# Order of heads and hyena channels, and where six modulation vectors are computed, in a two-layer hybrid mixer

## The chip, the cores and the metric

The kernel runs on one core of a Trainium2 chip. Its engines work beside each other: PE (TensorE) multiplies matrices into PSUM, DVE (VectorE), ACT (ScalarE) and POOL (GpSimd) do element work, and SP (SyncE) issues the DMAs that bring the weights from HBM. Each engine takes its own instructions in the order in which the program gives them and waits for the others by semaphores. The metric is the device time of one execution in microseconds (us), median of three runs.

## What is computed

Two layers over 256 latent and 256 context tokens of width 1024. Each layer has a token mixer of three branches and a mixture of 16 experts. Shift, scale and gate vectors (six per layer) come from a matrix product of two condition vectors with `w_mod`.

```python
mod  = split((sc     @ w_mod + b_mod), 6)     # latent tokens
modc = split( sc_ctx @ w_mod + b_mod,  6)     # context tokens
h    = modulate(rmsnorm(x, norm1_g), mod[0], mod[1])
dq, dk, dv, hy, sq, sk, sv, gt = split_in(h @ w_in)
y_diff = differential attention over dq, dk, dv      # 8 heads
y_hy   = hyena(hy): short conv, then FFT convolution with a computed filter
y_swa  = windowed attention with a sink over sq, sk, sv
y  = (sum of sigmoid(gate_b) * (y_b @ w_branch[b]) over the three branches) @ w_out
x  = x + mod[2] * y
h2 = modulate(rmsnorm(x, norm2_g), mod[3], mod[4])
x  = x + mod[5] * experts(h2)                        # top-k tokens of each expert
```

The second layer needs only the latent tokens behind its projections. A final RMSNorm closes the program.

## The kernel before, in words

The activations lie transposed in SBUF, channels on the partitions and tokens along the rows: 512 columns in the first layer, 256 (512 for keys and values) in the second.

**Blocks.** A mixer is a list of 116 blocks, made by `mixer` (L1371) and run by `run_blocks` (L984). A block is one slice of 128 columns of `w_in`, `w_branch` or `w_out`, loaded as `wraw` by SP, split into a high part `wh` (ACT) and a low part `wl` (half on POOL, half on DVE, L962), and multiplied with the high and low parts of its input (`hhi`, `hlo`, or `yb`, `mg`): 8 pieces of three matmuls (L456 and L459). The order of the list is: 24 blocks of heads (`diff_in`, L1418: q, k, v of each of 8 heads), 24 of hyena (`hyena_in`, L1403), four of the window attention (`swa_in`, L1477), then for each branch eight pairs of gate block and branch block (`branch`, L1428) with the other eight window blocks strewn in, and eight of the output. A block's last step (`evac`) takes the result from PSUM into a slot of the arena, a pool of SBUF slots, and may start a background task.

**Background tasks.** Each head, each hyena channel group and each window is a Python generator (`diff_gen` L1094, `hyena_gen` L1252, `swa_gen` L1189). `Background` (L286) keeps a queue of them, four live in the first layer and three in the second. Between the pieces of a block, `pump` (L366) steps those that its own clock model holds ready, as long as a credit of PE time lasts and ACT and DVE are not too far behind. All this happens while the program is built; what comes out is a fixed order for each engine. Two things force tasks without credit: `slot` (L391), where the arena has no free slot, and `drain` (L398), at a gate. The gates are the first block of each branch, whose `pre` (L1429) needs all tasks of its group finished, splits their results into `yb` and frees their slots. Before, the first gate drains heads and hyena together, and the first hyena block drains the task `filter` (L847), which computes the first layer's hyena filter in the background. Each hyena task reads that filter (`K`) and the transform matrices (`dft`) that follow it.

**Modulation vectors.** Vectors 0 and 1 of the first layer are computed in the setup. `mod_run` (L707) computes five more, (0,2), (0,3), (0,4), (1,0), (1,1) as (layer, vector), in the background of the first mixer: it loads 128 rows of 1024 columns of `w_mod` into `wm` and multiplies them on PE, four matmuls of 256 columns side by side in the array, 8 such groups a vector. Vector (0,5) is computed in the same way by a task that the fifth output block starts (`modA`, L1558) and that the expert stage drains (L1887). In the second mixer `mod_vec` (L727) computes three vectors on DVE instead: `ma = wm * sc + ma` for 8 pieces, and then four matmuls on PE that sum over the partitions by a selection matrix. `MODR` (L45) says how many blocks before the end of the second mixer this starts.

**Expert stages.** The weights of 16 experts come in pieces of 2 MB (`mw`) into buffers that the mixer gives up near its end and that the experts give back.

Of the kernel before, what the change touches and what calls it, by code (L numbers as in the profile page):

```python
# [17 lines left out]
OP = mybir.AluOpType  # L18
AX = mybir.AxisListType

D = 1024
KT = 8
# [13 lines left out]
COST = {"setup": 500.0, "filter": 60000.0, "mod": 15000.0, "modA": 5000.0, "modN": 5000.0, "diff": 9000.0, "hy": 10000.0, "swa": 4000.0, "post": 1000.0}  # L36
# [8 lines left out]
MODR = 58  # L45
# [8 lines left out]
MAGIC = 12582912.0  # L54
PI_IN = 3.1415925
# [352 lines left out]
class Kernel:  # L408
# [298 lines left out]
    def mod_run(self, vs, depth, pause, delay=3000.0):  # L707
        todo = [(l, v, k) for l, v in vs for k in range(KT)]
        raw = deque(self.mod_load(*todo.pop(0)) for _ in range(depth))
        yield wait(raw[0], delay=delay)  # L710
        for l, v in vs:
            acc = self.bank([128, 256], "m")
            for k in range(KT):
                w = raw.popleft()
                for c in range(4):
                    self.mm(acc[c * 32:(c + 1) * 32, :], self.sc[:, k, :], w[:, c * 256:(c + 1) * 256], k == 0, k == KT - 1, 4)
                w = None
                if todo:
                    yield wait(gate=self.room(a4=1))
                if todo:  # L720
                    raw.append(self.mod_load(*todo.pop(0)))
                yield wait(*list(raw)[:1], delay=pause)
            yield wait(acc, bank=0)
            yield from self.mod_out(l, v, acc)
            yield from self.mod_post(l, v)

    def mod_vec(self, vs):  # L727
        for l, v in vs:
# [19 lines left out]
            acc = None  # L748
            yield wait(p, bank=0)
            yield from self.mod_out(l, v, p, 30)  # L750
            yield from self.mod_post(l, v)
# [232 lines left out]
    def run_blocks(self, bl, ahead=2, first=3):  # L984
        nl = ns = first
        later = []
        for j, b in enumerate(bl):
# [11 lines left out]
            if self.bg.layer and len(bl) - 1 - j == MODR:  # L999
                self.bg.add("mod", lambda task: self.mod_vec([(1, v) for v in range(3, 6)]))  # L1000
# [251 lines left out]
    def hyena_gen(self, task, l, cs, u3):  # L1252
# [5 lines left out]
        yield wait(uv, gate=self.room(a2=2))  # L1258
# [112 lines left out]
    def mixer(self, l):  # L1371
# [28 lines left out]
        def pre_hy():  # L1400
            self.bg.drain("filter")

        def hyena_in():  # L1403
            w = 3 - ns
            for c0 in range(0, KT, w):
                cs = list(range(c0, c0 + w))
                for j in range(3):
                    for i, c in enumerate(cs):
                        def ev_c(p, cs=cs, c=c, i=i, j=j):
# [5 lines left out]
                        add(cols(win, O_HY + j * D + c * 128), H, nt, ev_c,  # L1415
                            *((pre_hy, ("filter",)) if c == 0 and j == 0 else ()))
# [11 lines left out]
        def branch(b, first, group):  # L1428
            def pre():  # L1429
# [3 lines left out]
                if first:  # L1433
                    self.bg.drain("hy")
                    self.K.pop(l)
                    self.dft = None
# [558 lines left out]
```

## Time and profile before

| what | value |
|---|---|
| median of three runs | 2637.61 us (2637.21 to 2639.09) |
| the profiled execution | 2639.09 us |
| its span, first to last instruction | 2637.3 us |
| PE busy | 2244.6 us, 85% |
| DVE busy | 1332.7 us, 51% |
| ACT busy | 883.4 us, 33% |
| POOL busy | 786.9 us, 30% |
| HBM read | 584.66 MB |
| mean granted TensorE clock | 0.937 |

The table gives the whole span; the shares are means over four stages: the first mixer (to about 1010 us), its experts (to 1544), the second mixer (to 2147), its experts. A share of busy time says little here. What a stage is bound by is read from the table of stretches below: which engine is near the length of the stretch, and whether the DMA share is near 1. In it a number in brackets with x counts instructions, and PEld is PE's loading of weights. PEclk is the mean of the clock granted to PE over the stretch, as a share of 2.4 GHz.

### The profile page before, as it was taken

Reading aid. Unit: us, or ns where it says so; the run is one execution under the profiler, and the core shown is the slowest. Engines: PE = TensorE matmul, PEld = TensorE weight load, DVE = VectorE, ACT = ScalarE, POOL = GpSimd, SP = SyncE. Lnnn points to the kernel's source line nnn. Section 1 sums busy time; section 2 is a strip of 40 time slices with the busy share of each in tenths; the row PEclk is TensorE's granted clock in tenths of the full one; section 3 lists DMA queues with packets and bytes.
Section 4 is the critical chain, followed back from the end, with each engine's and each line's share of the span. In section 5 each row is a group of like instructions: output and inputs, shape, how many; then the busy total and the mean of one; then the engine's idle time right before and its main releaser. Section 6 shows DMA issues by size and latency. Waiting matters only on the chain.

```text
span 2637.3 us, 38629 instructions
## 1 busy us (share of the span) xinstructions
PE 2244.6 (85%) x14938; PEld 1534.3 (58%) x14938; DVE 1332.7 (51%) x2899; ACT 883.4 (33%) x1933; POOL 786.9 (30%) x775
## 2 busy tenths in 40 slices
PE   6999998889989998898989799898888987666565
PEld 4777776767768774333333277787777863232223
DVE  4777788867662324223342158778788541111111
ACT  4445653345552332101110056553554430000001
POOL 2654225642333440001110055446554630000000
PEclk8999998989999999999999999998899988777888
DMA  8433342111213377999999942242365889999998
GB/s 293 119 120 112 96 128 89 52 53 52 69 57 88 92 251 288 373 407 400 356 379 403 404 158 80 72 121 80 100 180 160 253 308 409 409 409 409 409 409 305
DMA packets 390239, 590.31 MB, mean 224 GB/s; under 512 B 45948, under 2 KB 278056, under 8 KB 388776
## 3 DMA queue, kind: packets, MB, share of 16 engines
q1 hardware_dynamic: 390056, 587.84, 62.6%
q8 instruction: 118, 1.93, 0.3%
q14 instruction: 65, 0.53, 0.1%
HBM read 584.66 MB, written 3.15 MB: 223 GB/s over the span
## 4 chain that ended last, share of the span: by engine, by line
PE 40%; DMA 16%; DVE 13%; issue 3%; ACT 2%; SPq 2%; POOL 1%; ACTq 0%; DVEq 0%; POOLq 0%
PE p L457 38%; DMA mw<-in_moe_w_dram 15%; DVE t L260 3%; DVE arena L260 3%; PE p L468 2%; SPq L260 2%; DVE wl L260 2%; DVE qp L260 1%; DVE yb L260 1%; ACT wh L260 1%; ACT arena L260 1%; DVE ma L260 0%; DMA wraw<-in_w_in_dram 0%; DVE s L260 0%; DVE aT L260 0%
## 5 line engine op out<-in xcount | busy, mean ns | idle before, releaser
L457 PE MATMUL p<-mw,xg 128*32 128x256 f32 (+1 forms) x3072 | 406.7, 514 | 120.2 <-DMA mw<-in_moe_w_dram 120.0
L457 PE MATMUL p<-hhi,wh 128*128 128x512 f32 (+1 forms) x1344 | 496.7, 370 | 11.1 <-DVE arena L260 8.2
L457 PE MATMUL p<-hhi,wl 128*128 128x512 f32 (+1 forms) x1344 | 481.4, 358 | 26.9 <-DVE wl L260 26.4
L457 PE MATMUL p<-hlo,wh 128*128 128x512 f32 (+1 forms) x1344 | 476.6, 355 | 2.5 <-POOL hlo L260 1.4
L260 POOL TENSOR_TENSOR wl<-wraw,wh 128x512 fp32r<-128x512 f32 x232 | 330.9, 1427 | 460.2 <-ACT wh L260 365.9
L457 PEld LDWEIGHTS p<-mw,xg 128*32 128x32 f32 (+1 forms) x3072 | 137.3, 132 | 331.7 <-issue 203.7
L457 PEld LDWEIGHTS p<-hhi,wl 128*128 128x128 f32 x1344 | 258.3, 192 | 76.6 <-DVE wl L260 41.8
L457 PEld LDWEIGHTS p<-hhi,wh 128*128 128x128 f32 x1344 | 259.0, 193 | 49.3 <-issue 17.7
L457 PEld LDWEIGHTS p<-hlo,wh 128*128 128x128 f32 x1344 | 259.2, 193 | 30.3 <-POOL hlo L260 2.0
L260 ACT ACTIVATE wh<-wraw 128x1024 fp32r<-128x1024 f32 x232 | 242.1, 1053 | 43.2 <-PE p L457 12.1
L457 PE MATMUL p<-mw,aT 128*32 128x256 f32 (+3 forms) x1760 | 204.0, 483 | 59.3 <-DMA mw<-in_moe_w_dram 42.4
L260 DVE TENSOR_TENSOR wl<-wraw,wh 128x512 fp32r<-128x512 f32 x231 | 195.5, 846 | 60.1 <-ACT wh L260 58.9
L260 ACT ACTIVATE arena<-p 128x512 f32<-128x512 f32 (+1 forms) x212 | 106.0, 504 | 344.7 <-PE p L457 286.2
L260 ACT ACTIVATE yS<-p 32x256 f32<-32x256 f32 (+2 forms) x84 | 35.2, 419 | 499.3 <-PE p L457 465.8
L457 PE MATMUL p<-yb,wh 128*128 128x512 f32 (+1 forms) x768 | 197.1, 347 | 0.0
L260 POOL TENSOR_TENSOR sq<-sq,sq 128x512 f32<-128x512 f32 (+1 forms) x6 | 6.4, 1058 | 577.3 <-ACT sq L260 575.4
L457 PEld LDWEIGHTS p<-mw,aT 128*32 128x32 f32 (+1 forms) x1760 | 78.0, 134 | 167.9 <-issue 86.5
L260 DVE TENSOR_TENSOR s<-s,p 128x512 f32<-128x512 f32 (+1 forms) x32 | 17.7, 554 | 290.2 <-PE p L457 290.1
L260 DVE COPY yS<-p 32x512 f32<-32x512 f32 (+1 forms) x60 | 33.3, 556 | 244.5 <-ACT yS L260 244.5
L457 PE MATMUL p<-yb,wl 128*128 128x512 f32 (+1 forms) x384 | 133.2, 347 | 17.4 <-DVE wl L260 16.3
L457 PEld LDWEIGHTS p<-yb,wh 128*128 128x128 f32 x768 | 133.3, 195 | 15.0 <-issue 1.2
L260 ACT ACTIVATE arena<-p,t 128x512 f32<-128x512 f32 (+1 forms) x192 | 116.3, 612 | 65.2 <-DVE t L260 59.2
(235 smaller groups left out, 3506.0 us busy)
## 6 DMA issues: line engine op xcount, KB each, us to landing
mw<-in_moe_w_dram SPq DMA_DIRECT2D x173, 2048.0 KB, 19.3
wraw<-in_w_in_dram SPq DMA_DIRECT2D x152, 512.0 KB, 4.0
wm<-in_w_mod_dram SPq DMA_DIRECT2D x72, 512.0 KB, 4.5
mw<-in_moe_w_dram SPq DMA_DIRECT2D x40, 512.0 KB, 15.8
mw<-in_moe_w_dram SPq DMA_DIRECT2D x17, 1024.0 KB, 21.4
wraw<-in_w_branch_dram SPq DMA_DIRECT2D x32, 512.0 KB, 3.9
wm<-in_w_mod_dram SPq DMA_DIRECT2D x5, 2048.0 KB, 8.1
wraw<-in_w_in_dram SPq DMA_DIRECT2D x32, 256.0 KB, 3.3
```

Source lines behind the costliest of these rows:

```text
L260: return f(*args, **kw)
L457: self.nc.tensor.matmul(out, lhsT=lhsT, rhs=rhs, start=start, stop=stop, skip_group_check=tiles > 1)
L468: self.nc.tensor.transpose(out, in_, self.ident[:n, :n])
```

## The change

Three things change, all in the program that makes the order.

1. The blocks of heads and of hyena channels are dealt in turn by a table `ORDER`, one letter per head (`d`) or hyena group (`h`). In the first layer four heads come first, then `hhd hhd hhhh dd`; in the second they alternate, with four heads at the end. The hyena branch becomes the first of the three branches and the heads' branch the second, so that the first gate drains only hyena. The first hyena block no longer drains the filter; a hyena task itself waits until filter and transform matrices are there.
2. `mod_run` and its two tasks are gone. A new `mod_both` computes the vectors (0,2) to (0,5), (1,0) and (1,1) on DVE, in halves of 512 columns, for both condition vectors; it starts 62 blocks before the end of the first mixer.
3. The costs `modA` and `modN` and the two drains of these tasks are gone.

```diff
-MODR = 58
+MODR = (62, 58)
+ORDER = ("dddd" + "hhd" * 2 + "hhhh" + "dd", "dh" * 4 + "dddd")
...
-    def mod_run(self, vs, depth, pause, delay=3000.0):
...
-                for c in range(4):
-                    self.mm(acc[c * 32:(c + 1) * 32, :], self.sc[:, k, :], w[:, c * 256:(c + 1) * 256], k == 0, k == KT - 1, 4)
...
+    def mod_both(self, vs):
+        for l, v in vs:
+            p = None
+            for hf in range(2):
+                def load(k):
+                    t = self.sb("a2", [128, 512], name="wm")
+                    self.nc.sync.dma_start(t, self.A["w_mod"][l, k * 128:(k + 1) * 128, v * D + hf * 512:v * D + hf * 512 + 512])
+                    return t
+
+                yield wait(gate=self.room(a4=1, a2=3), bank=0)
+                acc = self.sb("a4", [128, 2, 512], name="ma")
+                ws = deque(load(k) for k in range(2))
+                for k in range(KT):
+                    yield wait(ws[0], acc, bank=0)
+                    w = ws.popleft()
+                    for s in range(2):
+                        sc = self.sc[:, k, s:s + 1]
+                        if k:
+                            self.stt(acc[:, s], w, sc, acc[:, s], OP.mult, OP.add)
+                        else:
+                            self.ts(acc[:, s], w, sc, None, OP.mult)
...
+                        self.mm(p[q * 32:(q + 1) * 32, :], self.sel[s], acc[:, s, c * 256:(c + 1) * 256], s == 0, s == 1, 4)
...
-            if self.bg.layer and len(bl) - 1 - j == MODR:
-                self.bg.add("mod", lambda task: self.mod_vec([(1, v) for v in range(3, 6)]))
+            if len(bl) - 1 - j == MODR[self.bg.layer]:
+                vs = [(1, v) for v in range(3, 6)] if self.bg.layer else [(0, v) for v in range(2, 6)] + [(1, 0), (1, 1)]
+                self.bg.add("mod", lambda task: (self.mod_vec if self.bg.layer else self.mod_both)(vs))
...
-        yield wait(uv, gate=self.room(a2=2))
+        yield wait(uv, gate=lambda: l in self.K and len(self.dft or ()) == 2 and self.room(a2=2)())
...
-        diff_in()
-        hyena_in()
+        parts = {"d": diff_in(), "h": hyena_in()}
+        for c in ORDER[l]:
+            next(parts[c])
...
-        branch(0, True, "diff")
-        branch(1, False, "hy")
+        branch(1, True, "hy")
+        branch(0, False, "diff")
...
-                if j == 4 and full:
-                    vs = [(l, 5)]
-                    self.bg.add("modA", lambda task: self.mod_run(vs, 2, 1300.0, 19000.0 if full else 11000.0))
...
-            self.bg.drain("modA")
...
-        self.bg.add("modN", lambda task: self.mod_run([(0, 2), (0, 3), (0, 4), (1, 0), (1, 1)], 1, 6000.0))
```

What this does to the order of the engines is seen at three places. In the names, `arena` is a slot, `ma` the accumulator of a modulation vector, `qp` a split query, `svt` transposed values, `t` a small statistic. First PE in the fifteenth block of the first mixer, before:

```order
L457 MATMUL p_1298<-wm_1303,sc_121 32x256 x4
L468 MATMUL p_1428<-cst_68,arena_576 128x128 x2
L457 MATMUL p_1421<-hhi_337,wh_1354 128x512
L457 MATMUL p_1421<-hlo_338,wh_1354 128x512
L457 MATMUL p_1421<-hhi_337,wl_1355 128x512
```

and now:

```order
L458 MATMUL p_1334<-kp_868,qp_1025 128x512
L458 MATMUL p_1334<-kl_869,qp_1025 128x512
L458 MATMUL p_1330<-hhi_337,wh_1241 128x512
L458 MATMUL p_1330<-hlo_338,wh_1241 128x512
L458 MATMUL p_1330<-hhi_337,wl_1242 128x512
```

The groups on `wm` have left the early blocks; there was about one in each.

Second DVE around block 66 of the first mixer, where the window tasks run, before:

```order
L260 TENSOR_TENSOR wl_6140<-wraw_5871,wh_6139 128x512
L260 SCALAR_TENSOR_TENSOR arena_87<-arena_87,p_6143 128x512
L260 TENSOR_TENSOR wl_6174<-wraw_5962,wh_6173 128x512
L260 STREAM_SHUFFLE sh_6206<-arena_574 128x256
L260 TENSOR_TENSOR arena_574<-arena_574,cst_68 128x256
L260 TENSOR_TENSOR wl_6212<-wraw_6095,wh_6211 128x512
```

and now:

```order
L261 COPY arena_574<-p_5910 128x128
L261 SCALAR_TENSOR_TENSOR ma_5748<-wm_5871,sc_121,ma_5748 128x512 x2
L261 COPY arena_572<-p_5920 128x512
L261 SCALAR_TENSOR_TENSOR ma_5748<-wm_5908,sc_121,ma_5748 128x512 x2
L261 TENSOR_REDUCE t_5960<-p_5941 128x1
L261 TENSOR_REDUCE t_5960<-p_5942 128x1
L261 TENSOR_TENSOR t_5960<-t_5960,nsink_409 128x2
L261 TENSOR_TENSOR t_5960<-t_5960,sink_408 128x2
L261 COPY arena_572<-p_5951 128x128
L261 TENSOR_TENSOR qp_5884<-arena_572,qp_5884 64x128 x2
L261 SCALAR_TENSOR_TENSOR ma_5748<-wm_5935,sc_121,ma_5748 128x512 x2
L261 TENSOR_TENSOR wl_5904<-wraw_5710,wh_5903 128x512
```

Accumulations of `ma` now stand between the steps of the window tasks, ahead of the next block's `wl`.

Third DVE at the gate of the third branch in the second mixer, between the evacuations of the blocks before and behind it, before:

```order
L260 SCALAR_TENSOR_TENSOR arena_11572<-arena_11572,p_16923 128x256
L260 TENSOR_TENSOR yb_16960<-arena_11573,yb_16960 128x256 x4
L260 TENSOR_TENSOR wl_16957<-wraw_16907,wh_16956 128x512
L260 SCALAR_TENSOR_TENSOR ma_16517<-wm_16933,sc_121,ma_16517 128x1024
L260 TENSOR_TENSOR wl_17012<-wraw_16946,wh_17011 128x512
```

and now, of which the first twelve rows of some sixty ahead of `yb` stand here:

```order
L261 SCALAR_TENSOR_TENSOR arena_11728<-arena_11728,p_16775 128x256
L261 TENSOR_TENSOR t_16716<-t_16716 128x2
L261 RECIPROCAL t_16716<-t_16716 128x2
L261 TENSOR_SCALAR arena_11728<-arena_11728,t_16716 128x512
L261 TENSOR_SCALAR arena_11729<-arena_11729,t_16716 128x512
L261 TENSOR_TENSOR qp_16721<-arena_11729,qp_16721 64x128 x2
L261 COPY arena_11728<-p_16832 128x128
L261 COPY arena_11729<-p_16852 128x512
L261 TENSOR_REDUCE t_16877<-p_16857 128x1
L261 TENSOR_REDUCE t_16877<-p_16858 128x1
L261 TENSOR_TENSOR t_16877<-t_16877,nsink_409 128x2
L261 TENSOR_TENSOR t_16877<-t_16877,sink_408 128x2
```

Steps of window tasks that stood among earlier blocks now stand at the gate, ahead of the split into `yb`.

## Rows read from the trace of the kernel before

**Rows 1.** Stretches: length; busy us of PE, PEld, DVE, ACT, POOL; PEclk, DMA, GB/s.

```profile
87.00:356.00 269.00, 259.84 (x1463) 198.58 (x1462) 202.87 (x482) 144.24 (x337) 120.80 (x149) 1.00 0.38 114
356.00:566.00 210.00, 175.75 (x936) 137.97 (x935) 173.56 (x305) 86.02 (x178) 104.01 (x85) 0.92 0.25 73
566.00:890.00 324.00, 309.30 (x1693) 240.13 (x1692) 183.28 (x442) 140.71 (x318) 110.77 (x105) 0.99 0.25 69
1010.00:1544.00 534.00, 469.72 (x2505) 194.18 (x2505) 169.38 (x416) 75.99 (x170) 46.64 (x72) 0.97 0.98 379
1579.00:1863.00 284.00, 245.67 (x1525) 215.40 (x1523) 222.82 (x457) 151.44 (x300) 150.20 (x131) 0.95 0.30 86
1863.00:2066.00 203.00, 185.49 (x1498) 165.11 (x1497) 169.68 (x310) 101.91 (x214) 94.42 (x90) 0.98 0.58 170
...
2160.00:2637.00 477.00, 303.61 (x3612) 145.73 (x3612) 62.64 (x170) 40.82 (x113) 2.20 (x3) 0.80 0.98 387
```

**Rows 2.** The same for instructions on `wm` alone, PE, PEld, DVE.

```profile
87.00:356.00 269.00, 16.61 (x208) 4.09 (x208) 0.00 (x0) 1.00 0.38 114
356.00:566.00 210.00, 7.03 (x88) 1.73 (x88) 0.00 (x0) 0.92 0.25 73
```

**Rows 3.** PE in order of time around one group on `wm`: start, duration, instruction.

```profile
107.23 0.40 PE L457 MATMUL p<-hlo,wh 128*128 128x512 f32 x1
107.46 0.40 PE L457 MATMUL p<-hhi,wl 128*128 128x512 f32 x1
107.79 0.64 PE L457 MATMUL p<-wm,sc 128*32 128x256 f32 x8
108.36 0.50 PE L457 MATMUL p<-hhi,wh 128*128 128x512 f32 x1
```

**Rows 4.** What PE waited for in 356 to 566: us, times, longest.

```profile
PE p L457 <- DVE wl L260: 10.8, 7, 2.8
...
PE p L457 <- POOL yf L260: 4.8, 1, 4.8
```

**Rows 5.** Instructions on `ma`: ns least/median/most, first and last start.

```profile
L260 DVE SCALAR_TENSOR_TENSOR ma<-wm,sc,ma x21: 1269/1280/2346, 1908.1 to 2075.7; 128x1024 f32<-128x1024 f32 x21
L260 DVE TENSOR_SCALAR ma<-wm,sc x3: 741/748/754, 1904.2 to 2031.8; 128x1024 f32<-128x1024 f32 x3
```

**Rows 6.** The same for `wl` on DVE, whole run.

```profile
L260 DVE TENSOR_TENSOR wl<-wraw,wh x231: 676/691/1779, 28.8 to 2141.2; 128x512 fp32r<-128x512 f32 x116
```

**Rows 7.** Groups of DVE instructions in 566 to 890: busy us, mean ns.

```profile
L260 DVE TENSOR_TENSOR wl<-wraw,wh 128x512 fp32r<-128x512 f32 x42 | 36.3, 866 | 36.9 <-ACT wh L260 36.4 <-DMA wraw<-in_w_branch_dram 0.3
```

**Rows 8.** Groups of DVE instructions, whole run.

```profile
L260 DVE TENSOR_TENSOR qp<-arena,qp 64x128 fp32r<-64x128 f32 x192 | 82.4, 429 | 41.7 <-ACT qp L260 36.5
L260 DVE TENSOR_REDUCE t<-p 128x1 f32<-128x512 f32 x128 | 82.0, 681 | 4.0 <-PE p L457 3.8
...
L260 DVE COPY arena<-p 128x512 f32<-128x512 f32 x66 | 44.9, 685 | 8.8 <-PE p L468 8.5
L260 DVE TENSOR_SCALAR arena<-arena,t 128x512 f32<-128x512 f32 x64 | 37.2, 623 | 1.2
...
L260 DVE TENSOR_TENSOR t<-t,nsink 128x2 f32<-128x2 f32 x48 | 18.8, 392 | 1.6
...
L260 DVE COPY arena<-p 128x128 f32<-128x128 f32 x48 | 13.8, 288 | 29.1 <-PE p L457 29.1
...
L260 DVE TENSOR_TENSOR yb<-arena,yb 128x256 fp32r<-128x256 f32 x12 | 11.0, 969 | 0.9 <-ACT yb L260 0.8
```

**Rows 9.** SP's queue around the end of the first mixer.

```profile
979.03 22.97 SPq L260 DMA_DIRECT2D wm<-in_w_mod_dram  x8
1006.79 55.12 SPq L260 DMA_DIRECT2D mw<-in_moe_w_dram  x17
```

**Rows 10.** Busy time of two stretches that hold a gate.

```profile
500.00:550.00 50.00, 36.44 (x171) 29.19 (x172) 36.38 (x48) 22.16 (x41) 36.11 (x30) 0.86 0.16 42
1760.00:1880.00 120.00, 97.06 (x652) 87.31 (x652) 93.27 (x161) 51.55 (x96) 70.78 (x57) 0.89 0.31 84
```

More of the change, by code (lines that the diff above doesn't have):

```diff
@@ L705, in mod_load @@
         return t
-    def mod_run(self, vs, depth, pause, delay=3000.0):
[L708 to L714, printed above, removed]
-                for c in range(4):
-                    self.mm(acc[c * 32:(c + 1) * 32, :], self.sc[:, k, :], w[:, c * 256:(c + 1) * 256], k == 0, k == KT - 1, 4)
[L717 to L725, printed above, removed]
     def mod_vec(self, vs):
@@ L750, in mod_vec @@
             yield from self.mod_out(l, v, p, 30)
+            yield from self.mod_post(l, v)
+    def mod_both(self, vs):
[18 more added lines that the diff above has]
+                            self.ts(acc[:, s], w, sc, None, OP.mult)
+                    w = None
+                    if k < KT - 2:
+                        yield wait(gate=self.room(a2=1), bank=0)
+                        ws.append(load(k + 2))
+                yield wait(acc)
+                if hf == 0:
+                    p = self.bank([128, 256], "m")
+                for s in range(2):
+                    for c in range(2):
+                        q = hf * 2 + c
+                        self.mm(p[q * 32:(q + 1) * 32, :], self.sel[s], acc[:, s, c * 256:(c + 1) * 256], s == 0, s == 1, 4)
+                acc = None
+            yield wait(p, bank=0)
+            yield from self.mod_out(l, v, p, 30)
+            p = None
             yield from self.mod_post(l, v)
@@ L1414, in ev_c @@
                                 self.bg.add("hy", self.hyena_task(l, cs, [st.pop(("u", q)) for q in range(3)]), 4)
-                        add(cols(win, O_HY + j * D + c * 128), H, nt, ev_c,
-                            *((pre_hy, ("filter",)) if c == 0 and j == 0 else ()))
+                        add(cols(win, O_HY + j * D + c * 128), H, nt, ev_c)
+                yield
         def diff_in():
@@ L1466, in branch @@
                 add(cols(win, O_GT + b * D + j * 128), H, nt, ev_g,
-                    *((pre, (group, "hy") if first else (group,)) if j == 0 else ()))
+                    *((pre, (group,)) if j == 0 else ()))
                 w = A["w_branch"][l, b]
@@ L1537, in pre_out @@
             self.bg.drain("mod")
-            self.bg.drain("modN")
             self.bg.arena = None
```

6 lines of the change are left out of this document (2 added, 4 removed).

## The prediction

> **What bounds the kernel now.** I read the run by stretches first. The table of busy time per stretch [rows 1] has seven stretches whose borders lie between blocks; a block is one 128-column piece of a weight, 24 matmuls, and I number the 232 blocks by the program (0 to 115 first mixer, 116 to 231 second), finding their times by counting 24 matmuls each in the PE timeline. 87 to 356 us is blocks 6 to 35, 356 to 566 blocks 36 to 53, 566 to 890 blocks 54 to 95, 1579 to 1863 blocks 122 to 167, 1863 to 2066 blocks 168 to 208. The reader is to see that PE sets the pace of the first mixer: 259.8 of 269 us busy, then 309.3 of 324. The exception is 356 to 566, the stretch of the hyena tasks: PE 175.8 of 210 at a granted clock of 0.92, a mean over its levels 1.2 and 2.4 GHz, while DVE has its densest stretch of the mixer, 173.6 us. Its waits [rows 4] name DVE (wl, 10.8 us) and POOL (yf, 4.8): weights whose low half stands behind background work, and chains that the gate of the first branch forces through with no block matmuls beside them. From 566 DVE is free for 43% of the time. The two expert stages are at DMA share 0.98, so a mixer that ends earlier hands its gain on.
>
> **Removed: the modulation matmuls of the first mixer.** In 87 to 566 there are 296 records of them [rows 2], 8 to a group, 37 groups of the 40 that five vectors make. A block's matmuls start 0.23 us apart; from the last one before a group (107.46) to the first one behind it (108.36) are 0.90 us [rows 3], so a group takes 0.67 us from PE. 40 x 0.67 = 27 us on the path, since PE is the bound there. The sixth vector's eight groups stand at the head of the first expert stage. They run mostly while PE waits for the routing chain on DVE anyway: I take 1 us (0 to 3). Its eight loads stand on SP from 979 to 1002 us, with the expert weights queued behind them from 1006.8 [rows 9]. Their 4.2 MB would be 11 us at the 379 GB/s of the stage [rows 1]; but the weights that fit ahead of the first expert are bounded by free buffers, and each later one by a buffer that an expert gives back, so I cost the bytes at nothing and keep 11 as the far end.
>
> **Added: six vectors on DVE.** 6 x 2 halves x 8 pieces x 2 streams = 192 instructions over 512 columns, 24 TENSOR_SCALAR and 168 SCALAR_TENSOR_TENSOR, between blocks 58 and 96 by the order. The nearest rows are the same instructions over 1024 columns in the second mixer: 0.748 and 1.280 us at the median, up to 2.346 [rows 5]. Half of that: 24 x 0.37 + 168 x 0.64 = 9 + 108 = 117 us. The upper bound takes what a DVE instruction with two SBUF inputs gives away here while POOL works: wl has a median of 0.691 us but a mean of 0.866 in this very stretch [rows 6, 7], 0.175 more. 9 + 168 x 0.815 = 146 us. I take 117, because most of the 21 instances sit at the median, and keep 146 for the range. On PE come 12 groups that sum the two streams, 12 x 0.67 = 8 us. 96 loads of 256 KB take the place of 48 of 512; on SP each can hold back the weight loads queued behind it until DVE has released its buffer, but a block's weights are issued two blocks or more ahead, so I cost that at nothing; if that cover is gone, each late load is a PE wait for wl.
>
> **Moved within the first mixer.** By the order the filter ends in block 24 (before: 20), the first hyena matmuls come in block 28 (before: 38), the last in 46 (before: 51), and the last head ends in 55 (before: 41); the sliding-window tasks run to 89 instead of 80. So some 20 us of DVE and, with the longer tail of windows, by an estimate 10 us of PE go past block 54. Of these 10 I count 5 as saved ahead of it, since the idle stretches there would have held the rest. The removed drain of the filter costs nothing: it is done four blocks before its first reader. Lost in 356 to 566 now: 34 us idle and 8% of 210 us at the lower clock, 17 us, together 51 [rows 1] (a mean clock of 0.92 is 8% below full). What is late next is a run inside block 36, where the evacuation finds no free arena slot and forces some 65 DVE instructions, by the kinds of [rows 8] about 30 us. The window that holds the forced gate of before has DVE at 36.4 of 50 us [rows 10], 73%; so 41 us, in which PE has 74 matmuls, most of a quarter of a block matmul's columns, by an estimate from the 0.23 us 12 us: 29 lost, 6 more for the clock, and some 9 at the gate of the first branch, where the split of its input still stands. 51 becomes 44: 7 us back.
> Blocks 3 to 53: -27 - 5 - 7 = **-39 us** (-48 to -25).
> Blocks 54 to 95: PE gets 309 + 8 + 10 = 327 and, with its 15 us of idle, needs 342. DVE gets 183 + 20 + 117 = 320. Two engines this full do not overlap perfectly; I add 6: 348 against 324, **+24 us** (+14, nearly free, to +46, where DVE is the bound: 183 + 20 + 146 = 349 at 94%, 370).
>
> **Moved within the second mixer.** Hyena and heads alternate, so the gate of the first branch has no hyena to force. 1760 to 1880, which holds that gate, has 23 us idle and 11% of 120 us at the lower clock, 36 lost [rows 10]; half remains, because waits for qp and yd and the split at the gate are still there: -18. But heads end at block 174 instead of 155, the windows start later, and five whole tasks and parts of two more are still open at the gate of the third branch, before block 208, where nothing was open. There DVE must run 10 REDUCE, 12 TENSOR_SCALAR, 5 x 2 qp, 6 wide and 7 narrow COPY: 6.8 + 7.5 + 4.3 + 4.1 + 2.0 = 25 us [rows 8], with 27 of 0.2 to 0.4 us and four splits some 34. At DVE's share of 85%, between the 73% of the other gate and a full engine: 40 us in which no block runs. The 134 short matmuls in it, by an estimate 16 us, and some 3 us of DVE waits are saved before it. -18 - 19 + 40 = **+3 us** (-12 to +18). The last expert stage, DMA share 0.98, moves with it.
>
> **Sum.** -39 + 24 - 1 + 3 = -13 us. The profiled execution took 2639.1 us around a span of 2637.3; the median of the three runs is 2637.6, so I set the 13 against that: **2624 us**, faster by 0.5%.
>
> **Rivals.** Only more than 0.2%, 5.3 us, can be told from no change.
> VectorE becomes the bound late in the first mixer: slower. For: 320 us of work in a stretch of 324, each wl behind two to eight of the new instructions, POOL with 111 us of its own there [rows 1]. Against: 21 instances of the instruction show few long ones. Price: 370 instead of 348, 2646 us. It decides the sign from about 0.79 us an instruction. The Trainium skill has this as a rule (SBUF — State Buffer, Who interferes with whom): a DVE instruction with two SBUF inputs contends for a shared port with a GpSimd instruction that reads SBUF, and the loser waits for the whole instruction. By that rule each of the 168 is exposed, and the sum would be this rival's; the trace bears it out for wl, whose slowest took 1.779 us [rows 6], less for the accumulations.
> The gate of the third branch costs what the first gate did: 34 us at 73% is 47, and the hyena stretch gives nothing back. +28 instead of +3: 2649 us, slower. For: the tasks there are chains over four engines. Against: they overlap three at a time.
> The forced run only changes place: block 36 costs as much as the gate did, the late stretch 30, the sum is near -1: 2637 us, no change.
> All gets smoother: -48, +14, -1, -6 makes -41: 2597 us. For: 51 us lost now in one stretch. Against: the forced runs that stand in the order.
>
> **How the numbers follow.** Forecast 0.38, smoother 0.15: faster 0.53. Only a change of place: same 0.15. VectorE-bound 0.22, the third gate 0.10: slower 0.32. The range, 2592 to 2662 us, takes in the forecast, the smoother case and the two slower ones, with the bounds of the accumulation's price and of the gate; about 1 in 10 lies beyond either end.
>
> **What would show it.** Right: no matmul on wm in the first mixer; blocks 6 to 53 in some 440 us instead of 479; blocks 54 to 95 in about 348 with DVE over 90% busy and ma at 0.65 us; a hole of about 40 us in the block matmuls before block 208, DVE-led; the hyena stretch of the second mixer without its gate. Wrong: ma near 0.8 us with PE waiting for wl through the late stretch (first rival); a hole beyond 50 us (second); the first half of the first mixer as long as before (third); PE waits for DMA there, which I costed at nothing.

## The result and the profile after

The changed kernel takes 2663.36 us (median of four runs, 2656.09 to 2673.31) against 2638.35 us of the kernel before beside it: ratio 1.0094, 95% interval 1.0079 to 1.011. Five more runs of it, beside later experiments, gave 2661.11 us (2658.37 to 2664.61), ratio 1.0089 (1.0073 to 1.0104). It is slower by 0.9%, where the prediction had it faster by 0.5%. The first median lies 1.4 us above the range, that of the five more runs 0.9 us inside it.

The profiled execution took 2663.28 us, 24.2 more than that of before. The stretches of after between blocks 6, 36, 54 and 96, and between blocks 122, 168 and 208, in the columns of [rows 1]:

```profile
88.30:345.40 257.10, 236.94 (x1196) 193.10 (x1195) 202.83 (x424) 124.78 (x270) 128.83 (x146) 0.98 0.23 68
345.40:542.90 197.50, 166.30 (x824) 135.49 (x822) 160.82 (x302) 99.09 (x224) 101.04 (x92) 0.92 0.18 49
542.90:908.20 365.30, 343.19 (x1887) 253.77 (x1886) 342.32 (x701) 146.55 (x341) 115.07 (x106) 0.99 0.44 130
1589.60:1859.40 269.80, 240.85 (x1508) 212.86 (x1507) 209.80 (x420) 142.59 (x275) 152.26 (x131) 0.97 0.32 91
1859.40:2078.20 218.80, 190.29 (x1513) 168.69 (x1511) 182.09 (x340) 113.15 (x241) 105.52 (x100) 0.97 0.51 150
```

The reader is to see three things. Blocks 6 to 53 take 455 us instead of 479 (first two rows). Blocks 54 to 95 take 365 instead of 324, and there PE and DVE are busy for 343 and 342 us: two engines at 94% at once. The second mixer exchanges one loss for another: blocks 122 to 167 are 17 us shorter than before (286.8 to 269.8), blocks 168 to 207 are 19 us longer (199.8 to 218.8). The rows from 1579 and to 2066 in [rows 1] do not hold quite these blocks: they begin at block 123 and end behind block 208.

Blocks 54 to 95 are where the loss is, so I worked out from both traces what TensorE does there: for every matmul the time from its start to the start of the next, summed by kind (us). The three kernels on the right are experiments that follow.

| matmuls, blocks 54 to 95 | before | after | mod_alone | order_alone | ma_first |
|---|---|---|---|---|---|
| block matmuls, up to the next start | 258.5 | 271.1 | 274.1 | 257.4 | 263.7 |
| sums of `ma` over the partitions | 0 | 12.5 | 13.1 | 0 | 11.9 |
| rows and router preparation behind a vector | 0 | 4.7 | 4.5 | 0 | 4.5 |
| all other background matmuls | 65.2 | 77.0 | 75.8 | 77.6 | 75.2 |
| sum | 323.7 | 365.3 | 367.5 | 335.0 | 355.3 |

Of the 41.6 us, 17 are matmuls that the vectors bring along. All other background matmuls take 12 more, but the records that this stretch has more of would take 6 at their mean times in before (as many are added in mod_alone, without the new order). The other 18 us are matmuls further apart. 7 of them are idle time of PE, which goes from 14.7 to 22.1 us; 11 stand in steps in which PE counts as busy. PE's own waits for `wl` are no longer than they were (us, times, longest; before, then after):

```profile
PE p L457 <- DVE wl L260: 11.8, 6, 4.2
...
PE p L458 <- DVE wl L261: 11.8, 11, 2.0
```

The instructions on `ma`, which answer to [rows 5]: least, median and most of a duration in ns.

```profile
L261 DVE SCALAR_TENSOR_TENSOR ma<-wm,sc,ma x189: 736/747/2371, 557.7 to 2125.4; 128x512 f32<-128x512 f32 x168, 128x1024 f32<-128x1024 f32 x21
L261 DVE TENSOR_SCALAR ma<-wm,sc x27: 477/486/1521, 556.4 to 2080.4; 128x512 f32<-128x512 f32 x24, 128x1024 f32<-128x1024 f32 x3
```

The median is 0.747 us, but the mean of the 168 over 512 columns is 0.895. The timeline shows the reason; DVE and POOL around 621 us, with start, duration and instruction:

```profile
621.52 1.29 POOL L261 TENSOR_TENSOR wl<-wraw,wh 128x512 fp32r<-128x512 f32 x1 [4.82 <-ACT wh L261]
621.60 2.43 DVE L261 SCALAR_TENSOR_TENSOR ma<-wm,sc,ma 128x512 f32<-128x512 f32 x2
...
627.19 1.41 DVE L261 SCALAR_TENSOR_TENSOR ma<-wm,sc,ma 128x512 f32<-128x512 f32 x2
628.51 1.28 DVE L261 TENSOR_REDUCE t<-p 128x1 f32<-128x512 f32 x2
```

Two accumulations in a row take 1.41 us, and the next instruction starts 1.32 us after the first, so one costs 0.66 us of the queue. Beside POOL's half of `wl` two take 2.43. Over the stretch, counted from the trace: 119 of the 168 lie beside no instruction of POOL and last 736 to 753 ns; 49 lie beside one, with a median of 1221 and up to 1798.

The sums on PE:

```profile
580.95 0.40 PE L458 MATMUL p<-hhi,wl 128*128 128x512 f32 x1
581.27 1.06 PE L458 MATMUL p<-ma,sc 128*32 128x256 f32 x8
582.26 0.50 PE L458 MATMUL p<-hhi,wh 128*128 128x512 f32 x1
```

A group of 8 records takes 0.99 us here. From the block matmul before it to the one behind it are 1.31 us, where around a group on `wm` it was 0.90 [rows 3]. The group on `ma` lies on two of the four column positions of the array, since it sums one half of a vector.

### The profile page after: what moved, and what is told of

Read it like the earlier page. It is cut to its first block, busy times and chain, and to the rows that moved or that the text cites. A ratio compares the mean times of both kernels' runs of the same rounds, so it can differ in the third digit from the quotient of the medians.

```text
span 2661.5 us, 38364 instructions
## 1 busy us (share of the span) xinstructions
PE 2229.0 (84%) x14650; PEld 1535.4 (58%) x14650; DVE 1481.7 (56%) x3091; ACT 882.5 (33%) x1933; POOL 798.1 (30%) x775
## 4 chain that ended last, share of the span: by engine, by line
PE 42%; DVE 30%; DMA 19%; issue 4%; ACT 3%; POOL 1%; SPq 1%; DVEq 0%; ACTq 0%; POOLq 0%
PE p L458 39%; DMA mw<-in_moe_w_dram 17%; DVE arena L261 9%; DVE t L261 6%; DVE ma L261 5%; DVE wl L261 3%; PE p L469 3%; DVE qp L261 2%; DMA wm<-in_w_mod_dram 2%; SPq L261 1%; DVE yc L261 1%; ACT arena L261 1%; ACT wh L261 1%; DVE yb L261 1%; DMA wraw<-in_w_branch_dram 0%
## 5 line engine op out<-in xcount | busy, mean ns | idle before, releaser
L261 POOL TENSOR_TENSOR wl<-wraw,wh 128x512 fp32r<-128x512 f32 x232 | 343.8, 1483 | 398.8 <-ACT wh L261 333.2
L261 ACT ACTIVATE yS<-p 32x256 f32<-32x256 f32 (+2 forms) x84 | 35.2, 419 | 498.4 <-PE p L458 479.2
L261 DVE SCALAR_TENSOR_TENSOR ma<-wm,sc,ma 128x512 f32<-128x512 f32 (+1 forms) x189 | 176.2, 972 | 9.5 <-DMA wm<-in_w_mod_dram 9.1
```

The lines of the kernel that those rows point to most:

```text
L261: return f(*args, **kw)
```

## The experiments

Theory 1 was the prediction's first rival: VectorE is the bound late in the first mixer. Theory 2: the new order makes the loss. Two more came from the results. All times are medians.

| kernel | us | ratio to before (95%) |
|---|---|---|
| mod_alone | 2654.73 | 1.0057 (1.0041 to 1.0073) |
| order_alone | 2639.2 | 1.0003 (0.9992 to 1.0015) |
| ma_first | 2647.99 | 1.0026 (1.0014 to 1.0037) |
| heads_first_2 | 2655.91 | 1.0057 (1.0037 to 1.0076) |
| sums_joint | 2673.57 | 1.0128 (1.0105 to 1.0151) |
| mod_later | 2674.81 | 1.0141 (1.0118 to 1.0163) |
| no_run | 2674.63 | 1.0136 (1.0108 to 1.0163) |
| alone_joint | 2675.32 | 1.014 (1.0116 to 1.0163) |
| wl_sooner | 2673.03 | 1.0122 (1.0106 to 1.0137) |
| paced | 2673.89 | 1.0121 (1.0106 to 1.0136) |
| wl_dve | 2668.03 | 1.0099 (1.0082 to 1.0116) |
| alone_paced | 2649.63 | 1.0036 (1.0022 to 1.0049) |
| after_again | 2661.11 | 1.0089 (1.0073 to 1.0104) |
| first_wl_dve | 2668.18 | 1.0117 (1.0094 to 1.0139) |
| before_wl_dve | 2629.98 | 0.9968 (0.9958 to 0.9979) |
| before_wl_all | 2605.34 | 0.9871 (0.9841 to 0.9901) |
| alone_best | 2613.24 | 0.9915 (0.9899 to 0.9932) |
| order_wl | 2633.52 | 0.9984 (0.9971 to 0.9996) |

### Each part alone: mod_alone and order_alone

```diff
 # mod_alone: before, with
-MODR = 58
+MODR = (62, 58)
-    def mod_run ...  and its two tasks
+    def mod_both ...
 # order_alone: after, with mod_run and its tasks as before
```

> The kernel before with the six vectors on VectorE alone; heads, hyena and branches stand as before. Theory 1 (VectorE is the bound of the late stretch): blocks 3 to 53 give back about 27 us, blocks 54 to 95 grow by about 41 us as in the changed kernel (324 to 365), so +10 to +15, 2648 to 2653 us. Theory 2 (the new order makes the loss, by the run in block 36 and the gate of the third branch): without the order the vectors gain, -27 and +14, about 2624 us.

> The changed kernel with the vectors of the first mixer on TensorE again, as before; only the order and the branches are new. Theory 1: the late stretch is bounded by TensorE again and grows by no more than the 10 us of moved matmuls, the second mixer costs +2 to +5, the first half 0 to +7: 2640 to 2655 us. Theory 2: the order carries all of the loss and the vectors gave something back: 2670 us or more.

Blocks 3 to 53 and 54 to 95 of mod_alone, in the columns of [rows 1]:

```profile
63.90:536.20 472.30, 420.76 (x2107) 344.30 (x2107) 376.24 (x777) 235.87 (x517) 246.97 (x259) 0.95 0.22 61
536.20:903.80 367.60, 343.01 (x1884) 253.53 (x1882) 338.56 (x688) 145.00 (x338) 116.22 (x104) 0.99 0.44 129
```

and of order_alone:

```profile
62.50:552.00 489.50, 446.84 (x2437) 342.28 (x2437) 375.46 (x764) 228.46 (x493) 244.85 (x255) 0.98 0.34 101
552.00:887.00 335.00, 319.93 (x1779) 248.44 (x1778) 203.06 (x510) 154.12 (x361) 110.49 (x108) 0.99 0.25 68
```

In before these two stretches take 504.4 and 323.7 us, and in after 479.2 and 365.3. The first of them, before and after:

```profile
61.50:565.90 504.40, 460.07 (x2524) 353.97 (x2524) 398.12 (x833) 242.51 (x536) 245.94 (x258) 0.97 0.33 99
...
63.70:542.90 479.20, 424.17 (x2106) 345.25 (x2105) 382.79 (x765) 235.22 (x513) 247.99 (x258) 0.95 0.21 61
```

The vectors alone give 32 and take 44; the order alone gives 15 and takes 11, and its second mixer is as long as that of before. So the vectors make most of the loss, and theory 2 falls. The order is worth nothing by itself. The two gains in blocks 3 to 53, 32 and 15, are together only 25. The two losses in blocks 54 to 95, 44 and 11, are together only 42. So about 8 us of the loss belong to neither part alone.

### Is it VectorE? ma_first

```diff
-                        if k:
+                        if k > 7:
                             self.stt(acc[:, s], w, sc, acc[:, s], OP.mult, OP.add)
-                        else:
+                        elif not k:
```

> The changed kernel with only the first 24 of the 192 instructions on ma in the first mixer: the 168 accumulations are left out, so the vectors are not computed; loads, sums over partitions and order of the blocks stay. Theory 1: blocks 54 to 95 fall from 365 us to about 330, and the time to about 2630 us. Theory 2: the late stretch is long for another reason (moved window tasks, waits for loads), and the time stays above 2650 us.

Blocks 54 to 95:

```profile
539.40:894.70 355.30, 338.49 (x1888) 257.14 (x1888) 213.63 (x536) 146.99 (x341) 111.09 (x106) 0.98 0.45 134
```

The kernel leaves out the 168 accumulations, so it does not compute the vectors; loads and sums stay. VectorE loses 129 us of work and the stretch 10 (365.3 to 355.3), where theory 1 had put it at 330. The time, 2648 us, lies between the two forecasts. It is then PE that is busy for 338 of 355 us. Theory 1 falls as it stood: VectorE is not the only bound there. From this came theory 3: what the change adds to TensorE sets the pace.

### Less on TensorE, or the same work elsewhere: sums_joint, mod_later, alone_joint

```diff
 # sums_joint: both halves are kept, and then
+            for s in range(2):
+                for q in range(4):
+                    self.mm(p[q * 32:(q + 1) * 32, :], self.sel[s], accs[q // 2][:, s, q % 2 * 256:q % 2 * 256 + 256], ...)
 # mod_later: after, with
-MODR = (62, 58)
+MODR = (46, 58)
 # alone_joint: mod_alone, with sums_joint and MODR = (50, 58)
```

> The changed kernel, but the sums over partitions of a vector wait for both halves and run as 8 matmuls over four positions of the array, as the groups on wm did, instead of twice 4 over two positions. Measured so far, start to start: 26.5 us for 40 groups on wm (0.66 us each), 12.5 us for 12 groups on ma (1.04). Theory 3 (TensorE still sets the pace late in the first mixer, and what the change adds to it there counts): the sums fall from 12.5 to 8 us, and the time by 4 to 5 us, to 2658. Theory 1 (VectorE is the bound there): the accumulations are the same 192, nothing is gained, 2663 us.

> The changed kernel with the vectors started 46 instead of 62 blocks before the end of the first mixer, so that a part of the accumulations falls on blocks 96 to 107, where VectorE had 25 of 92 us to do. Theory 1: VectorE is relieved of about 50 us in blocks 54 to 95, and the time falls by 25 us or more, to 2638 or less. Theory 3: the matmuls added and moved stay (about 28 us), only the waits for wl that VectorE makes go, 10 us at most: 2653 us.

> The kernel before with the vectors alone on VectorE, started 50 blocks before the end of the first mixer, and with joint sums. Measured with start 62 and halved sums: 2654.7 us, -30 us in blocks 3 to 53 and +44 in 54 to 95. Theory 3: 4.5 us for the sums and up to 10 for the waits come back: about 2641 us. Theory 1: VectorE has room from start 50 on, 2630 us or less.

The size of the term was right: in the whole late stretch the sums of sums_joint take 7.9 us instead of 12.5, 0.66 a group. One pair of groups there:

```profile
604.91 0.40 PE L458 MATMUL p<-hhi,wl 128*128 128x512 f32 x1
605.24 1.07 PE L458 MATMUL p<-ma,sc 128*32 128x256 f32 x16
606.24 1.09 PE L458 MATMUL p<-arena,svt 128*64 128x128 f32 x16
```

Yet the kernel got slower, by 10 us or more: from the starts of block matmuls to the next starts, blocks 54 to 107, it went from 336.8 to 345.3 us, and PE's waits for `wl` in blocks 54 to 95 went from 11.8 to 19.9 us. What TensorE saved it waited for, and more. Theory 3 alone falls as well. In mod_later blocks 54 to 95 shrank by 3 us and the next twelve grew by 15:

```profile
537.10:899.20 362.10, 335.71 (x1852) 254.09 (x1852) 304.69 (x638) 147.44 (x341) 113.29 (x106) 0.99 0.37 111
899.20:979.70 80.50, 75.83 (x326) 57.37 (x324) 69.60 (x91) 18.54 (x24) 29.21 (x18) 0.96 0.60 196
```

Blocks 96 to 107 take 65.3 us in before, 5.4 each, with PE busy all the time and VectorE for a quarter of it:

```profile
889.60:954.90 65.30, 65.30 (x290) 54.09 (x289) 16.05 (x24) 18.07 (x24) 27.92 (x18) 1.00 0.41 129
```

In mod_later VectorE's half of `wl` stands behind up to eight accumulations, and a block of 5.4 us no longer hides them. An engine that is idle in the table can still be late for the one instruction that counts. alone_joint shows the same (74.5 us for these twelve) and took 2675 us where 2641 were forecast.

### Where the instructions stand: wl_sooner, paced, alone_paced

```diff
 # wl_sooner
-                if k >= LATER[self.bg.layer] and later:
+                if k >= (LATER[self.bg.layer] if self.bg.layer or j < 54 else 3) and later:
 # paced
-                    yield wait(ws[0], acc, bank=0)
+                    yield wait(ws[0], acc, bank=0, delay=2000.0)
 # alone_paced: mod_alone with sums_joint, wl_sooner and paced
```

Theory 4, from the waits of mod_later: `wl` stands behind bursts of accumulations.

> The changed kernel, but from block 54 on the DVE half of the next block's wl is put behind the fourth piece of a block instead of behind the seventh. Theory 4: it is not the share of VectorE that costs, but that wl stands behind four to eight accumulations (0.74 us each, 1.26 where an instruction of POOL lies beside it) with some 1.4 us left until its first reader; three pieces (2.1 us) more of cover take most of that: block matmuls of blocks 54 to 107 from 337 us to about 327, the time to 2653 us. Theory 1 (VectorE full): the same work on the same engine, 2663 us.

> The changed kernel with a pause of 2.0 us of TensorE time between two steps of a vector, so that two to six accumulations stand between two wl instead of two to eight, and the last vector ends in block 104 instead of 95. Theory 4: fewer behind one another, but also in blocks 96 to 104, where each wl waited for nothing: -8 and +5, about 2660 us. Theory 1: 20 us of VectorE work leave blocks 54 to 95, 2645 us.

> The kernel before with the vectors alone on VectorE (start 62 blocks before the end), sums joint over both halves, the pause of 2.0 us and the sooner wl of the other two runs. Measured without these: 2654.7 us, of which -30 in blocks 3 to 53 and +44 in 54 to 95 (16 of it block matmuls that wait, 13 sums, 5 row matmuls, 10 moved). Theory 4: sums 4.5 and waits 12 come back: about 2638 us, as the kernel before. Theory 1: 2650 us or more.

In wl_sooner the block matmuls of blocks 54 to 107 came down to 325.3 us, as theory 4 had it (327). But all other matmuls there went from 94.4 to 111.8: the sums on `ma` and the chains of the window tasks are held up instead, and the time is 2673 us, not 2653. Theory 4 names a true wait and not the bound. paced moved 15 us of VectorE's work out of blocks 54 to 95 and gained nothing there (366.0 us). Together with the shorter sums and the sooner `wl`, and without the new order, it helps: alone_paced has 353.3 us there against 367.6 in mod_alone, and is 5 us faster than it, where 16 were forecast. Which of the three edits does it, no run tells.

### The floor of the first half: no_run, first_wl_dve

```diff
 # no_run
-ORDER = ("dddd" + "hhd" * 2 + "hhhh" + "dd", ...)
+ORDER = ("dddhddhhhdhhdhhd", ...)
 # first_wl_dve: after; split_block in blocks 20 to 51
+        if later is not None and self.own:
+            c = KT
```

> The changed kernel with another deal of heads and hyena groups in the first mixer, dddhddhhhdhhdhhd, with which no block of the first half holds more than 44 background matmuls (the changed kernel: 74 in block 36). If the forced run in block 36 is why the two parts of the change gave 23 us together in blocks 3 to 53 where they gave 30 and 14 alone: 15 to 20 us come back, 2645 us. If the work of that run only stands elsewhere then: less than 5 us, 2660 us.

> The changed kernel, but in blocks 20 to 51 VectorE makes the whole of wl and POOL none. If VectorE's own work is the floor of that stretch: 32 times 0.4 us more on it, blocks 3 to 53 grow from 479 to about 490 us. If what POOL does beside it is: VectorE is no busier (as late in the mixer, where taking wl from POOL left it with 335 us instead of 342), POOL falls by some 45 us, and blocks 3 to 53 shrink to about 470 us.

Block 36 of after, which holds the forced run, and block 207 with the hole before block 208 of the second mixer:

```profile
345.40:387.00 41.60, 27.05 (x122) 21.61 (x120) 33.88 (x86) 20.18 (x63) 9.76 (x13) 0.76 0.09 26
2043.30:2078.20 34.90, 26.64 (x233) 20.75 (x231) 27.67 (x73) 20.63 (x55) 7.16 (x10) 0.95 0.24 65
```

Block 36 takes 41.6 us, but 12.9 of them hold its own matmuls, one of which waits 4.8 us for `wl`. The run itself, in which no block matmul starts, lasts 28.7 us, where the prediction had 41. The hole before block 208 lasts 30.3 us, with VectorE busy for 25.1 of them; the prediction had 34 of 40. Blocks 3 to 53 of no_run, which has no such run:

```profile
62.90:540.20 477.30, 421.63 (x2108) 340.81 (x2107) 381.72 (x778) 235.97 (x515) 243.17 (x258) 0.96 0.21 61
```

477.3 us against 479.2 in after and 476.3 in after_again: taking the run away gives nothing there. Blocks 54 to 95 of no_run grow to 378.6 us, and the kernel is 11 us slower or more. Every kernel without the vectors in its first half and with POOL's half of `wl` takes 471 to 479 us there, in whatever deal. first_wl_dve takes 472.2, between its two forecasts and nearer the second; VectorE is no busier (382.2 us) although it makes the whole of 32 `wl`. Block 36 takes 12.9 us in it, so the forced run is gone there as well.

### heads_first_2 and after_again

```diff
-ORDER = (..., "dh" * 4 + "dddd")
+ORDER = (..., "dddddddd" + "hhhh")
```

> The changed kernel, but in the second mixer all eight heads stand ahead of the hyena groups, as before; the hyena branch still leads. By the order nothing is forced at the third gate then. If the hole before block 208 costs its own 32 us: the time falls by 32 less what the hyena stretch had gained (23), to about 2654 us, and without the gate of heads and hyena at the first branch perhaps to 2640. If the hole only holds work that would stand elsewhere, the time stays at 2663 us or above.

> The changed kernel itself, unchanged, for more runs. If its time is 2663 us as the median of the first four says, the five variants at 2673 to 2675 us are slower than it by 10 us; if the first four were low by chance, it comes out at 2668 to 2675 and they are equal to it.

In heads_first_2 the hole is gone, blocks 168 to 207 in one row:

```profile
1880.00:2080.40 200.40, 181.20 (x1473) 160.65 (x1473) 165.66 (x307) 97.45 (x205) 93.31 (x87) 0.98 0.57 166
```

From block 116 to block 231 it takes 598.7 us, after 600.5, before 598.2. Its 5 us against after_again lie within its own spread (2647 to 2662). The deal of the second mixer is worth nothing either way. after_again settles that the variants at 2673 to 2675 us are truly slower than after.

### What POOL costs VectorE: wl_dve, before_wl_dve, before_wl_all, alone_best, order_wl

```diff
 # split_block
-        self.tt(b.wl[:, c:], b.raw[:, c:], h[:, c:], OP.subtract, self.nc.gpsimd)
+        if c < KT:
+            self.tt(b.wl[:, c:], b.raw[:, c:], h[:, c:], OP.subtract, self.nc.gpsimd)
 # wl_dve: c = KT in blocks 54 to 97 of after; before_wl_dve: 3 to 51 of before;
 # alone_best: 3 to 107 of alone_paced; order_wl: 3 to 51 of order_alone
 # before_wl_all: before, with
-WCUT = (4, 4)
+WCUT = (8, 8)
```

> The changed kernel, but in blocks 54 to 97 VectorE makes the whole of wl and POOL none of it: POOL loses 42 instructions of some 1.5 us, VectorE gets about 25 us of subtraction. If instructions of POOL are what makes an accumulation 1.26 us instead of 0.745 (49 of 168 in the changed kernel lie beside one): the mean falls from 0.90 in that stretch to 0.80 or less and 15 of the 25 us are given back; the time goes up by 5 to 15 us, 2670 us. If the long ones have another cause, the mean stays at 0.90 and the time goes to 2685 us.

> The kernel before, but in blocks 3 to 51 VectorE makes the whole of wl and POOL none. By the first reading VectorE gets 20 us more in a stretch where it is busy 79% and TensorE 91%: blocks 3 to 53 grow from 504 to about 510 us, 2643 us. By the second they shrink to about 495 us, 2630 us, which would beat both kernels.

> The kernel before with the whole of wl on VectorE in both mixers. In blocks 3 to 51 alone this gave 8 us (2630 against 2638 us). If POOL's half costs VectorE as much everywhere: nothing more late in the first mixer, where VectorE is busy 57%, and 5 to 10 us in the second mixer, where it is busy 78 to 84%: 2622 to 2628 us. If not: the second mixer grows by the 116 times 0.5 us added to VectorE, 2640 us or more.

> The vectors alone on VectorE with joint sums, pause and sooner wl (2649.6 us so far), and the whole of wl on VectorE in blocks 3 to 107. If the reading holds: 8 us in the first half and up to 10 late, 2632 to 2640 us; then VectorE has just room for the vectors. If not, 2650 us or more.

> The new order alone with the vectors on TensorE (2639 us so far), and the whole of wl on VectorE in blocks 3 to 51. If its 8 us add to the order: 2631 us. If both only reach the same floor of blocks 3 to 53 (487 us with wl alone, 490 with the order alone): 2639 us.

Groups on DVE in blocks 54 to 95 of wl_dve (busy us, mean ns):

```profile
L261 DVE SCALAR_TENSOR_TENSOR ma<-wm,sc,ma 128x512 f32<-128x512 f32 x168 | 132.3, 830 | 0.7 <-DMA wm<-in_w_mod_dram 0.4
L261 DVE TENSOR_TENSOR wl<-wraw,wh 128x1024 fp32r<-128x1024 f32 x43 | 54.5, 1268 | 0.4 <-ACT wh L261 0.3
```

and the stretch itself:

```profile
542.90:912.00 369.10, 343.41 (x1888) 257.45 (x1887) 334.84 (x700) 145.69 (x341) 56.63 (x64) 0.98 0.43 128
```

The mean of an accumulation falls from 0.895 to 0.830 us, not quite to the 0.80 forecast (31 instead of 49 lie beside an instruction of POOL). `wl` on VectorE grows from 33.1 to 54.5 us, and VectorE is busy for 334.8 us, 7.5 less than in after: twice as much of `wl`, and less time. The stretch itself is 4 us longer, so this does not mend the changed kernel.

On the kernel before it does. before_wl_dve gains 17 us in blocks 3 to 53 (504.4 to 487.1) and loses 7 of them again in blocks 54 to 95 (323.7 to 331.1); its 2630 us are what the second reading had forecast. In before_wl_all POOL makes none of `wl` anywhere. Whole runs: `wl` and the engines' busy time of before,

```profile
PE 2244.6 (85%) x14938; PEld 1534.3 (58%) x14938; DVE 1332.7 (51%) x2899; ACT 883.4 (33%) x1933; POOL 786.9 (30%) x775
L260 POOL TENSOR_TENSOR wl<-wraw,wh 128x512 fp32r<-128x512 f32 x231 | 328.6, 1423 | 460.2 <-ACT wh L260 365.9 <-issue 47.0 <-PE p L457 12.9
L260 DVE TENSOR_TENSOR wl<-wraw,wh 128x512 fp32r<-128x512 f32 x231 | 195.5, 846 | 60.1 <-ACT wh L260 58.9 <-DMA wraw<-in_w_branch_dram 0.3
```

and of before_wl_all:

```profile
PE 2213.9 (86%) x14938; PEld 1517.8 (59%) x14938; DVE 1352.7 (52%) x2899; ACT 881.9 (34%) x1933; POOL 493.6 (19%) x544
L260 DVE TENSOR_TENSOR wl<-wraw,wh 128x1024 fp32r<-128x1024 f32 x231 | 302.9, 1313 | 55.9 <-ACT wh L260 54.8
```

VectorE does 107 us more of `wl` (195.5 to 302.9) and is busy only 20 us longer: its other instructions, the same in number, take 87 us less of it. In this profile the largest gain is in the second mixer, blocks 119 to 167 before,

```profile
1561.00:1863.20 302.20, 263.24 (x1624) 230.63 (x1623) 231.79 (x473) 161.16 (x314) 165.90 (x147) 0.95 0.31 89
```

and in before_wl_all:

```profile
1538.50:1809.70 271.20, 251.32 (x1615) 221.86 (x1614) 229.76 (x466) 153.75 (x300) 93.26 (x89) 1.00 0.34 96
```

VectorE is no busier, POOL by 73 us less, the granted clock is 1.00 instead of 0.95, and the blocks take 31 us less. PE waits longer for `wl` there (12.2 us instead of 7.4) and less for VectorE's `yd` and `qp` and POOL's `yf` (1.9 instead of 18.4). So it is the background chains that come sooner, and not `wl`; whether by VectorE's shorter instructions or by POOL's free time, no run separates. before_wl_all takes 2605.34 us, 1.3% under the kernel before and past its forecast of 2622 to 2628. Its profiled execution (2589.7) was the fastest of its four by 15 us, so the rows above show more gain than the median has. alone_best, the vectors with POOL out of the first mixer's `wl`, takes 2613.24; its second mixer is that of before. Its blocks 3 to 53 and 54 to 95:

```profile
62.30:524.00 461.70, 417.27 (x2124) 340.13 (x2124) 384.10 (x791) 237.20 (x523) 188.72 (x207) 0.97 0.23 65
524.00:862.00 338.00, 325.52 (x1835) 253.39 (x1834) 301.52 (x629) 143.82 (x331) 53.70 (x63) 0.97 0.42 125
```

The second is 15 us less than in alone_paced (353.3). before_wl_all takes 490.0 and 316.3 us there and 65.3 in the twelve blocks behind, alone_best 68.6: with POOL out of `wl` the vectors on VectorE give 28 us and take 22 and 3, so by these two profiles moving them is worth a few us at best, and by the medians before_wl_all is the faster. order_wl has 482.7 us in blocks 3 to 53 where order_alone has 489.5: the two add in part.

## Why the prediction was wrong, step by step

The forecast was -13 us and the profiled execution took 24 more. 14 us of the difference lie in blocks 3 to 53, where two gains were added that do not add, and 18 in blocks 54 to 95, where the change costs PE more time than the sum had. Most of the rest lies ahead of block 3 (2.2) and behind block 231 (2.6), to which the prediction gave nothing.

**Removed matmuls, -27: right.** mod_alone gives 32 in blocks 3 to 53; 26.5 are the groups on `wm` by the start-to-start sums of before and 4.2 the rows and the router preparation behind a vector, which moved along.

**The moves in the first mixer, -5 and -7: right alone, wrong together.** order_alone gives 15. With the vectors gone too, blocks 3 to 53 give 25 in all, not 39. The run in block 36 was priced too long (41 us forecast, 28.7 measured) and is not the reason, by no_run; in order_alone block 36 takes 12.0 us, so the order by itself makes no such run, and that the 12 forecast come near its 15 is in part luck. The step that failed is adding the two gains: VectorE, busy 79% there before, is busy 80% after, while PE falls from 91 to 89%. A part of this floor goes with POOL's half of `wl`: without it the stretch falls by 17 us on before (504.4 to 487.1), by 11 on alone_paced (472.4 to 461.7) and by 4 to 7 on after. What makes the rest stays open.

**Blocks 54 to 95, +24: 42.** In the prediction's own terms PE was to be busy 18 us longer and idle 6 us longer. It is busy 34 us longer (309.0 to 343.2) and idle 7 (14.7 to 22.1): the overlap was sized right, and the work of PE is the term that failed. The sums: 8 forecast, 12.5 measured, since the price came from groups on four positions of the array and these lie on two. The rows and router preparation behind each vector: not counted, 4.7; they are instructions of a moved step. Moved windows: 10 forecast, 6 at the mean times of before (10 in order_alone). What is left, some 11 us, are steps between matmuls that grew while PE counts as busy; background work stands between block matmuls 104 times instead of 82, but what each of these costs, and how much of it VectorE makes, stays open.

**The price of an accumulation, 0.64: nearly right alone, wrong beside POOL.** A pair takes 1.32 us of the queue when POOL is idle. The stretch held 203.1 us of VectorE's work without vectors (order_alone; the prediction had 203) and 342.3 with them: 139 for the 192 instructions, against 117 chosen and 146 as the far end. (The rival was said to decide the sign from 0.79 us an instruction; with the prediction's own 94% in 361 us it is 0.76.) I took the median of 21 instances of the second mixer, where the mean of `wl` in this very stretch [rows 7] said what POOL adds. That the 21 show few long ones was a misreading: ten of them lie beside POOL, and their mean is 1.482 us against the median of 1.280.

```profile
L260 DVE SCALAR_TENSOR_TENSOR ma<-wm,sc,ma 128x1024 f32<-128x1024 f32 x21 | 31.1, 1482 | 2.6 <-DMA wm<-in_w_mod_dram 2.6
```

The Trainium skill (SBUF — State Buffer, Who interferes with whom) says that a DVE instruction with two SBUF inputs and a GpSimd instruction that reads SBUF shut each other out for a whole instruction. The trace bears it out: 0.745 us alone, 1.22 in the median and up to 1.80 beside POOL.

**The first rival** had the right place and sign, with DVE over 90% busy in that stretch as forecast, and its 370 us for the stretch are near the 365 measured; its sum, 2646, missed the 14 us of the first half. But it had not the whole mechanism. The long wait of PE for `wl` that was to show it is not there: 11.8 us before and after. By ma_first, VectorE's accumulations account for 10 of the 42 us; without them the stretch still takes 355 us, with PE busy for 338. That less on PE (sums_joint) and an earlier `wl` (wl_sooner) gave nothing fits two engines that bound the stretch together, at 94% each, but no run shows it: in none is PE relieved of all that the change adds.

**The loads, nothing: right** for the order as it stood; PE waited for no DMA in blocks 54 to 95, and VectorE for `wm` 0.7 us.

**The second mixer, +3: 2.3** from block 116 to 231, in part by luck. The hole before block 208 cost 32 us more than before (40 forecast), the blocks ahead of it gave 36 back (37 forecast), and blocks 208 to 231, at nothing in the forecast, took 6 more. The second rival falls. **The first expert stage,** -1, did not move: 544.2 us from block 115 to block 116, before 544.1.

## What to carry to other kernels

Two edits that each gain in a stretch, or each lose, are priced together and against its second-busiest engine; here -32 and -15 made -25, and +44 and +11 made +42. Work that is moved is priced where it lands, with all that follows it (sums, row copies, preparations) and with its neighbours on the other engines: the mean duration in that stretch, not the median from elsewhere. Sharing elementwise work between VectorE and POOL is worth a trial without POOL: here VectorE made the whole of `wl` for 20 us more of busy time, and the kernel took 33 us less.

## What was not expected of the hardware

POOL's share of an elementwise step can cost VectorE nearly as much as doing it. 231 instructions of POOL on `wl` took it 328.6 us; without them VectorE did twice the columns of `wl` in 20 us more of busy time, where `wl` itself takes 107 us more. The stretching is not confined to instructions with two inputs from SBUF: the 24 TENSOR_SCALAR on `ma` last 477 to 488 ns alone (18) and 1.27 us in the mean beside POOL (6, up to 1.52). The Trainium skill (SBUF — State Buffer, Who interferes with whom) has this too, for one-input instructions that use both port pairs; the trace agrees in the 0.52 ns a column that this instruction takes (482 to 748 ns from 512 to 1024 columns), half of an accumulation's 1.04.

Eight records of a 32-column matmul take 0.66 us of the queue on four column positions and about 1 us on two.
